# Log-softmax backward on one core: three tiles loaded, then three stored, on one queue; result in place of dy; stores of whole rows

**Chip, cores, metric.** One core of one Trainium2 chip, the pair's other core idle. The metric is device time in microseconds (us) of one execution, median of several runs. All runs compared here are of the fast state.

## The reference

```python
def reference(y, dy):                      # both (8, 1024, 8192) float32
    softmax_x = np.exp(y)
    sum_dy = np.sum(dy, axis=-1, keepdims=True)
    return (dy - softmax_x * sum_dy).astype(np.float32)
```

As a matrix that is 8192 rows of 8192 numbers: 64 tiles of 128 rows, 4 MiB each for y, dy and the result.

## The kernel before

```python
    yp = ctx.enter_context(tc.tile_pool(name="yp", bufs=3))
    dyp = ctx.enter_context(tc.tile_pool(name="dyp", bufs=2))
    op = ctx.enter_context(tc.tile_pool(name="op", bufs=2))
    # ... psum (2 buffers), stats; H = 4096, CD = 2048
    for i in range(n_tiles):
        # ...
        nc.sync.dma_start(out=dy_t[:], in_=dy_f[sl])
        nc.sync.dma_start(out=y_t[:], in_=y_f[sl])
        nc.vector.tensor_reduce(out=s_t[:], in_=dy_t[:], ..., negate=True)
        for h in range(n_half):
            o_t = op.tile([P, H], fp32)
            for q in range(n_q):
                # ... c = h * n_q + q; e_t in PSUM = exp(y_t[:, cs]) on ScalarE
                nc.vector.scalar_tensor_tensor(      # e_t * s_t + dy_t
                    out=o_t[:, q * CD : (q + 1) * CD], in0=e_t[:], scalar=s_t[:], in1=dy_t[:, cs], ...)
            nc.sync.dma_start(out=out_f[sl][:, h * H : (h + 1) * H], in_=o_t[:])
```

All DMAs go out from SyncE, in one order, on one queue. A scheduler settles that order; it isn't the source's. In the kernel before it is, from the second tile on: dy of tile i+1, the two half stores of tile i, y of tile i+1, dy of tile i+2, and so on.

## Time and profile before

| | before |
|---|---|
| time, median of 3 (range) | 1925.06 us (1923.62 to 1926.75) |
| moved | 805.3 MB: two thirds read, one third written |
| mean rate | 418 GB/s |
| DMA queue, share of 16 engines' time | 99.5% |
| VectorE, ScalarE busy | 59%, 25% |

The DMA bounds it: no compute engine is near full, and the queue's packets fill nearly all the time. The prediction below shows the lines.

Two orders of issue are told apart here by the **lead** of a transfer: the time from its issue on SyncE to its first packet on a DMA engine. The trace gives both ends. A short lead means that the queue was nearly empty when the transfer was put into it. The 16 engines don't run in step, so a lead has a value for the fastest engine (which comes first to the new transfer, so has the shortest) and for the slowest. The packet records carry no engine number. Packets are put to an engine by time: a packet starts some 3 ns before the end of the one ahead of it on the same engine. Where two engines end together this can mix them up, so figures by single engine are good to a few cases, not exact.

### The profile page before, as it was taken

The numbers are of one execution on the slowest core, as the hardware profiler recorded it, in microseconds if no ns is written. First come the engines' busy times: TensorE is split into PE (matmuls) and PEld (weight loads), VectorE is DVE, ScalarE is ACT, GpSimd is POOL, SyncE is SP. The second block draws the span as 40 slices with busy tenths as digits, with TensorE's granted clock in tenths as the row PEclk, the third lists the DMA queues.
The fourth block names the chain that finished last, engine by engine and source line by source line (L and its number), as shares of the span: only waits on it lengthen the run. The fifth ranks groups of instructions, "written<-read, shape, count | busy, mean of one in ns | idle before, by whom it ended". The sixth has DMA issues, their size and how long they took to land.

```text
span 1924.6 us, 1253 instructions
## 1 busy us (share of the span) xinstructions
DVE 1134.1 (59%) x320; ACT 477.5 (25%) x257; POOL 0.2 (0%) x4
## 2 busy tenths in 40 slices
DVE  5657556465564655756657556475564655646555
ACT  1322313223132131221322313223132231321312
POOL 0000000000000000000000000000000000000000
DMA  9999999999999999999999999999999999999997
GB/s 414 426 432 415 425 424 420 423 420 423 420 414 425 422 420 423 414 424 420 421 423 414 420 422 421 418 422 422 418 426 420 418 425 425 414 425 414 425 425 318
DMA packets 36874, 805.40 MB, mean 418 GB/s; under 512 B 4096, under 2 KB 4096, under 8 KB 4096
## 3 DMA queue, kind: packets, MB, share of 16 engines
q1 hardware_dynamic: 36864, 805.32, 99.5%
q14 instruction: 10, 0.08, 0.0%
HBM read 536.87 MB, written 268.44 MB: 418 GB/s over the span
## 4 chain that ended last, share of the span: by engine, by line
DMA 61%; DVE 29%; ACT 6%; issue 2%; SPq 1%; DVEq 0%; ACTq 0%
DMA y_t<-in_y_dram 61%; DVE o_t L70 29%; ACT e_t L67 6%; SPq L78 1%; DVEq L104 0%; ACTq L67 0%; SPq L51 0%; SPq L50 0%
## 5 line engine op out<-in xcount | busy, mean ns | idle before, releaser
L70 DVE SCALAR_TENSOR_TENSOR o_t<-e_t,s_t,dy_t 128x2048 f32<-128x2048 f32 x256 | 584.1, 2344 | 770.0 <-ACT e_t L67 770.0
L67 ACT ACTIVATE e_t<-y_t 128x2048 f32<-128x2048 f32 x256 | 476.2, 1877 | 1436.2 <-DMA y_t<-in_y_dram 1372.4
L53 DVE TENSOR_REDUCE s_t<-dy_t 128x1 f32<-128x8192 f32 x64 | 555.2, 8676 | 12.9 <-DMA dy_t<-in_dy_dram 12.9
L67 ACT ACT_TABLE_LOAD x1 | 1.3, 1283 | 0.7 <-PEq L93 0.7
L93 POOL MEMSET const-bfloat16-1.0<- 128x1 bf16 x1 | 0.1, 102 | 0.0
L93 POOL MEMSET const-uint8-127<- 128x1 uint8 x1 | 0.1, 102 | 0.0
L93 POOL MEMSET const-float32-0.0<- 128x1 f32 x1 | 0.1, 99 | 0.2 <-issue 0.2
L93 POOL MEMSET const-float32-1.0<- 128x1 f32 x1 | 0.1, 99 | 0.0
## 6 DMA issues: line engine op xcount, KB each, us to landing
dy_t<-in_dy_dram SPq DMA_DIRECT2D x64, 4096.0 KB, 27.8
y_t<-in_y_dram SPq DMA_DIRECT2D x64, 4096.0 KB, 18.3
out_dram<-o_t SPq DMA_DIRECT2D x128, 2048.0 KB, 8.7
```

Of the source, the lines that this page charges most:

```text
L53: nc.vector.tensor_reduce(out=s_t[:], in_=dy_t[:], axis=mybir.AxisListType.X, op=mybir.AluOpType.add, negate=True,)
L67: nc.scalar.activation(e_t[:], y_t[:, cs], mybir.ActivationFunctionType.Exp)
L70: nc.vector.scalar_tensor_tensor(out=o_t[:, q * CD : (q + 1) * CD], in0=e_t[:], scalar=s_t[:], in1=dy_t[:, cs], op0=mybir.AluOpType.mult, ...
L78: nc.sync.dma_start(out=out_f[sl][:, h * H : (h + 1) * H], in_=o_t[:])
L93: nc = _bacc.Bacc("TRN2", target_bir_lowering=False, num_devices=1)
```

## The change

The intent: fewer changes between loading and storing, larger store packets, no output buffers.

```diff
-    n_half = 2
-    ...
-    yp = ... bufs=3;  dyp = ... bufs=2;  op = ... bufs=2
+    BATCH = 3
+    dyp = ctx.enter_context(tc.tile_pool(name="dyp", bufs=BATCH + 1))
+    yp = ctx.enter_context(tc.tile_pool(name="yp", bufs=2))
...
+    first = n_tiles % BATCH
+    starts = [0] * bool(first) + list(range(first, n_tiles, BATCH))
+    for b, e in zip(starts, starts[1:] + [n_tiles]):
+        done = []
+        for i in range(b, e):
+            # load dy_t, load y_t, s_t = -sum(dy_t), as before
+            subtract_scaled_exp(nc, psum, y_t, dy_t, s_t[:], CD)   # writes into dy_t
+            done.append((sl, dy_t))
+        for sl, dy_t in done:
+            nc.sync.dma_start(out=out_f[sl], in_=dy_t[:])
```

More of the change, by code (lines that the diff above doesn't have):

```diff
@@ L8, with subtract_scaled_exp @@
 from concourse.bass import ts
+ACT_EXP = mybir.ActivationFunctionType.Exp
+ALU = mybir.AluOpType
+def subtract_scaled_exp(nc, psum, y_part, dy_part, neg_sum, width):
+    total = y_part.shape[-1]
+    for c in range(0, total, width):
+        e_t = psum.tile([128, width], mybir.dt.float32, name="e_t")
+        nc.scalar.activation(e_t[:], y_part[:, c : c + width], ACT_EXP)
+        nc.vector.scalar_tensor_tensor(
+            out=dy_part[:, c : c + width],
+            in0=e_t[:],
+            scalar=neg_sum,
+            in1=dy_part[:, c : c + width],
+            op0=ALU.mult,
+            op1=ALU.add,
+        )
 @with_exitstack
@@ L27 @@
     N, D = y_f.shape
-    assert N % P == 0, (N, P)
     n_tiles = N // P
-    n_half = 2
-    H = D // n_half
-    n_q = 2
-    CD = H // n_q
-    assert CD * 4 * 2 <= 16 * 1024, "psum budget"
-    yp = ctx.enter_context(tc.tile_pool(name="yp", bufs=3))
-    dyp = ctx.enter_context(tc.tile_pool(name="dyp", bufs=2))
-    op = ctx.enter_context(tc.tile_pool(name="op", bufs=2))
+    assert N == n_tiles * P
+    CD = 2048
+    BATCH = 3
+    dyp = ctx.enter_context(tc.tile_pool(name="dyp", bufs=BATCH + 1))
@@ L40 @@
+    yp = ctx.enter_context(tc.tile_pool(name="yp", bufs=2))
     psum = ctx.enter_context(tc.tile_pool(name="psum", bufs=2, space=bass.MemoryType.PSUM))
     stats = ctx.enter_context(tc.tile_pool(name="stats", bufs=8))
-    for i in range(n_tiles):
-        sl = ts(i, P)
-        dy_t = dyp.tile([P, D], fp32)
-        y_t = yp.tile([P, D], fp32)
-        s_t = stats.tile([P, 1], fp32)
-        nc.sync.dma_start(out=dy_t[:], in_=dy_f[sl])
-        nc.sync.dma_start(out=y_t[:], in_=y_f[sl])
-        nc.vector.tensor_reduce(
-            out=s_t[:],
-            in_=dy_t[:],
-            axis=mybir.AxisListType.X,
-            op=mybir.AluOpType.add,
-            negate=True,
-        )
-        for h in range(n_half):
-            o_t = op.tile([P, H], fp32)
-            for q in range(n_q):
-                c = h * n_q + q
-                cs = slice(c * CD, (c + 1) * CD)
-                e_t = psum.tile([P, CD], fp32)
-                nc.scalar.activation(
-                    e_t[:], y_t[:, cs], mybir.ActivationFunctionType.Exp
-                )
-                nc.vector.scalar_tensor_tensor(
-                    out=o_t[:, q * CD : (q + 1) * CD],
-                    in0=e_t[:],
-                    scalar=s_t[:],
-                    in1=dy_t[:, cs],
-                    op0=mybir.AluOpType.mult,
-                    op1=mybir.AluOpType.add,
-                )
-            nc.sync.dma_start(out=out_f[sl][:, h * H : (h + 1) * H], in_=o_t[:])
@@ new lines @@
+    first = n_tiles % BATCH
[3 more added lines that the diff above has]
+        for i in range(b, e):
+            sl = ts(i, P)
+            dy_t = dyp.tile([P, D], fp32, name="dy_t")
+            nc.sync.dma_start(out=dy_t[:], in_=dy_f[sl])
+            y_t = yp.tile([P, D], fp32, name="y_t")
+            nc.sync.dma_start(out=y_t[:], in_=y_f[sl])
+            s_t = stats.tile([P, 1], fp32, name="s_t")
+            nc.vector.tensor_reduce(
+                out=s_t[:], in_=dy_t[:], axis=mybir.AxisListType.X, op=ALU.add, negate=True
+            )
+            subtract_scaled_exp(nc, psum, y_t, dy_t, s_t[:], CD)
+            done.append((sl, dy_t))
+        for sl, dy_t in done:
+            nc.sync.dma_start(out=out_f[sl], in_=dy_t[:])
```

## The prediction

> **What bounds the kernel now.** First the page, busy shares and queue: is an engine near full, or the DMA?
>
> ```profile
> span 1924.6 us, 1253 instructions
> DVE 1134.1 (59%) x320; ACT 477.5 (25%) x257; POOL 0.2 (0%) x4
> DMA packets 36874, 805.40 MB, mean 418 GB/s; under 512 B 4096, under 2 KB 4096, under 8 KB 4096
> q1 hardware_dynamic: 36864, 805.32, 99.5%
> ```
>
> VectorE has 41% of the span free, ScalarE 75%. The one queue's packets fill 99.5% of 16 engines' time. So DMA bounds it, and only three things can help: fewer bytes, cheaper packets, or the 0.5%. The bytes stay: 64 tiles x 3 x 4 MiB = 805.3 MB.
>
> Second, the queue's waits and the DMA issues: does a late issue starve the queue?
>
> ```profile
> SPq L78 <- DVE o_t L70: 1736.8, 128, 27.1
> dy_t<-in_dy_dram SPq DMA_DIRECT2D x64, 4096.0 KB, 27.8
> y_t<-in_y_dram SPq DMA_DIRECT2D x64, 4096.0 KB, 18.3
> out_dram<-o_t SPq DMA_DIRECT2D x128, 2048.0 KB, 8.7
> ```
>
> SyncE sits 1737 us before stores, but that costs nothing in the steady state: a y load moves in some 9.7 us (below) and lands 18.3 us after its issue, so other packets were always ahead of it. "DMA y_t" as 61% of the chain means the same: compute waits for the queue.
>
> Third, bytes per stretch of time: first a stretch of pure loading, then three of the tail.
>
> ```profile
> 4.00:30.00 26.00, 14.16 (x4) 6.39 (x4) 0.00 (x0) 1.00 0.99 430
> 1903.00:1905.00 2.00, 0.00 (x0) 0.00 (x0) 0.00 (x0) 1.00 0.04 16
> 1905.00:1913.00 8.00, 5.06 (x3) 5.97 (x4) 0.00 (x0) 1.00 0.01 2
> 1913.00:1924.00 11.00, 4.07 (x2) 1.47 (x1) 0.00 (x0) 1.00 0.90 381
> ```
>
> The last two columns are DMA share and GB/s. Loads alone reach 430; the span's mean is 418. And from 1903 to 1913 the queue is empty: the last y has come, its tile is being computed, and nothing is left to move until its stores.
>
> Fourth, the trace's single DMA packets (start, duration, size), which no printed view shows; I sorted them by engine. A 32 KiB load packet takes 1213 ns and the next starts 1209.5 ns after it (27.1 GB/s per engine, 433 for 16). A 16 KiB store packet takes 611 ns, one every 607. But of each run of 16 store packets (two stores of half a row, 8 packets per engine each) the last is on average 400 ns too long, the one before 85, the third from the end 12; the first load packet after it is 116 too long. Small excesses and gaps at the same two borders of a cycle (stores to loads 0.02 us, loads to stores 0.06, the last load packets 0.04) bring it to **0.73 us per engine and change of direction and back**. Whole cycles agree: loads 19.58 us where 16 x 1.2095 = 19.35, stores 10.29 where 16 x 0.607 = 9.71, together 0.81 too long, the rest of it semaphore packets and single packets inside. Inside the runs nearly nothing is lost, not even at the border between the two half stores (0.3 ns). So part of the "99.5% busy" is packets that stand still while stores give way to loads. That is what there is to win.
>
> **What the Trainium skill says.** "DMA: Bandwidth & Descriptors", section "Where 436 GB/s comes from", puts the ceiling of 16 engines at 435.2 GB/s; the load runs at 433 agree, so within a run nothing is left. "HBM Reference", section "Specifications (TRN2)", says that a core streaming alone gets about 425 GB/s, bounded by its DMA engines; 418 here is below that, with loads and stores mixed. "DMA: Bandwidth & Descriptors", section "Queues, rings and completion order", says that on each DMA engine descriptors are consumed in ring order; the packets agree: each engine's runs of loads and stores follow the order of issue, so the program decides how often the direction changes. No page gives a cost for a change of direction; the 0.73 us is this trace's. The same page, section "Latency and other measured facts", puts an HBM access at 0.2 us on average and 2 us at high load; that the engine waits about one HBM read when it goes from reading SBUF to reading HBM would fit 0.73, but is only my reading.
>
> **The change part by part.**
> 1. Directions. Before, each tile is two loads, then its two half stores: 64 store runs, 63 of them followed by loads. After, the instruction order has one single tile, then 21 batches of three: 22 store runs, 21 followed by loads. 42 fewer x 0.73 = **30.6 us** off the path, as the queue is the path.
> 2. The tail. Before, the engines idle 9.6 us (largest gap per engine, mean of 16) between the last y packet and the last stores. After, when the last y is in, two stores (19.4 us) stand in the queue. The last tile needs 13.4 us from its last packet: 2.3 to the start of exp, 1.9 for exp, 9.13 for the four VectorE instructions (the trace's last tile: packets end at 1903.6, VectorE at 1917.1). So its store joins a queue with 6 us left: **9.6 us** saved.
> 3. Packets. 1024 store packets of 607 ns per engine become 512 of 32 KiB. If these go like loads (1209.5), 512 x (1214 - 1209.5) = **2.3 us**. 64 fewer semaphore packets per engine of some 6 ns: **0.4 us**.
> 4. In place. The result goes to dy's tile; same instruction, shapes and count (256 of 2344 ns). VectorE's 1134 us stay beside the transfers. Cost 0, if the waits hold, which I walk through, with 9.7 us per 4 MiB and time 0 at the last packet of a batch's first y: dy_b to 9.7, y_b 19.4, dy_c 29.0, y_c 38.7, stores a, b, c to 48.4, 58.1, 67.7. The issue of store c: 38.7 + 13.4 = 52.1, before 58.1: **6 us in hand**, the tightest place. The next dy_b needs store a complete (48.4 + 2.3 = 50.7, before 52.1), the next dy_c needs store b (60.4, with four transfers queued behind it by then). y_c waits for the exps of tile a (11 us after y_a; three transfers are queued). Store a then waits for VectorE at 13.4, store b at 32.8. VectorE: sum for c 32.8 to 41.5, exp for c ready at 42.9. Start: the first store is issued at 33.7 with dy and y of tile 1 queued to about 41. Nothing starves.
>
> Sum: 30.6 + 9.6 + 2.3 + 0.4 = 42.9; 1924.6 - 42.9 = 1881.7 in the profile, and some 0.5 more in the timed median (1925.06): **1882 us**, 2.2% faster, at 428 GB/s.
>
> **The rivals.**
> - Lost time goes with bytes stored or number of DMAs, not with changes of direction. Then only the tail and packet terms come: 1925 - 12 = 1913, within 2%. Against it: the clean inside of the runs, and the 0.3 ns at the half-store border, where a DMA ends and no direction changes. For it: nothing before has runs of more than 16 store packets.
> - The queue starves: SyncE issues in order, and y_c, store a and each dy wait in it for compute or for stores in place. Each us lost per batch costs 21 us; 2 us would eat the gain (1924). For it: only 6 us in hand, where the former kernel stored from buffers of its own. Against: the walk above, and stalls of 2 us wouldn't fit in its numbers.
> - The change of direction costs more after 12 MiB of stores than after 4 (a write backlog that must drain). At 1.5 us instead of 0.73 it costs 21 x 0.77 = 16 us: 1898, within 2%. Against: a backlog would lengthen packets through the run, and they stay at 611 up to the last three.
> - Less than thought remains: the engines drift apart less, and borders get cheaper. 1876.
>
> **Range and chances.** 2% faster is 1886.6, only 4.6 us above my sum, so the sizes matter, not the direction. The largest term (30.6) is a mean over 63 borders, and I give it 20% either way (6 us); the tail term is sure to 2 us. Range 1871 to 1897. Faster by over 2%: 0.68; within 2%: 0.31; slower: 0.01.
>
> **What would show each step.** Right: some 428 GB/s; no empty stretch between the last y and the last stores; the last store packets of a batch long by some 0.5 us and 21 such places, not 63; stores of 4096 KB landing 37, 28 and 18 us after issue in a batch (from the walk), so 28 as the median; q1 share still at 99%. Wrong: a DMA share below 0.9 inside batches (starving), store packets that lengthen within a run (writes saturate), a border that costs over 1 us, or a 32 KiB store packet well over 1213 ns.

## The result

The changed kernel takes **1871.67 us** (median of 4, 1871.40 to 1872.19) against 1925.34 us (4 runs) before. Ratio 0.972, interval 0.9706 to 0.9733: faster by 2.8%. A ratio is the mean time of one kernel's fast runs over that of the other's in the same rounds, so not quite the ratio of the medians quoted. The time lies inside the predicted range (1871 to 1897), at its lowest edge: the gain is 53.7 us where 43 were forecast.

The page of the changed kernel (span, engines, packets, queue):

```profile
span 1870.2 us, 1067 instructions
DVE 1136.0 (61%) x320; ACT 477.5 (26%) x257; POOL 0.2 (0%) x4
DMA packets 27656, 805.38 MB, mean 431 GB/s; under 512 B 3072, under 2 KB 3072, under 8 KB 3072
q1 hardware_dynamic: 27648, 805.32, 100.0%
```

The same bytes at 431 GB/s in place of 418, VectorE as before. The queue's share went from 99.5 to 100.0%: by this share there was half a per cent to win, and 2.8% was won. So this share doesn't tell how much can be won; more below.

Its waits of SyncE and its DMA issues (count, KB, median us from issue to landing):

```profile
SPq L75 <- DVE dy_t L20: 867.4, 64, 20.8
SPq L67 <- DMA y_t<-in_y_dram: 583.6, 21, 29.4
SPq L67 <- ACT e_t L19: 178.4, 21, 8.5
SPq L65 <- DMA out_dram<-dy_t: 100.8, 20, 5.7
dy_t<-in_dy_dram SPq DMA_DIRECT2D x64, 4096.0 KB, 45.2
y_t<-in_y_dram SPq DMA_DIRECT2D x64, 4096.0 KB, 36.3
out_dram<-dy_t SPq DMA_DIRECT2D x64, 4096.0 KB, 27.7
```

The price of working in place is there (SyncE waits 101 us for stores before it loads dy again), but it costs nothing, as every transfer is issued so long before its turn: 27.7 to 45 us to landing, where 4 MiB move in 9.7. In the kernel before, a half store landed 8.7 us after its issue, of which some 4.9 are its own packets and 0.35 the way from the last packet to the semaphore (median). Little is left, 3.3 us on the slowest engine and 1.0 to 1.5 on most of the others: it was issued when the queue was nearly dry.

Bytes per stretch at the end of the changed kernel (last columns DMA share, GB/s):

```profile
1838.00:1856.00 18.00, 11.80 (x5) 7.44 (x4) 0.00 (x0) 1.00 1.01 434
1856.00:1866.00 10.00, 0.00 (x0) 0.00 (x0) 0.00 (x0) 1.00 0.87 374
1866.00:1870.00 4.00, 0.00 (x0) 0.00 (x0) 0.00 (x0) 1.00 0.06 25
```

The empty 10 us between the last y and the last stores are gone, as forecast. In their place is a smaller loss: most engines end within 1 us of each other, but the last one 3.8 us after the middle one. In the kernel before, the empty stretch let the late engine catch up, and the last packets ended within 0.2 us of each other.

And the bubbles? Time by which single packets took longer than the usual 1213 ns (32 KiB) or 611 ns (16 KiB), added up, per engine, from the trace's packet records:

```
                  stretched packets   of which store packets
before                 44.9 us              34.5 us
changed                 4.5 us      (sizes are equal; last stores of runs: under 0.1 us)
```

By the prediction's rule, 21 changes of direction at 0.73 us should have left 15 us. They left almost nothing: over the 20 later batches together, the first load after the stores is too long by under 0.1 us per engine, and so is the last store. So a change from stores to loads is free in the changed kernel. It wasn't the change of direction that cost.

### The profile page after: what moved, and what is told of

The parts are those of the page before. It is cut to its first block, busy times and chain, and to the rows that moved or that the text cites. A ratio compares the mean times of both kernels' runs of the same rounds, so it can differ in the third digit from the quotient of the medians.

```text
span 1870.2 us, 1067 instructions
## 1 busy us (share of the span) xinstructions
DVE 1136.0 (61%) x320; ACT 477.5 (26%) x257; POOL 0.2 (0%) x4
## 4 chain that ended last, share of the span: by engine, by line
DMA 61%; DVE 13%; ACT 5%; SPq 1%; issue 0%; DVEq 0%; ACTq 0%
DMA y_t<-in_y_dram 61%; DVE dy_t L20 13%; ACT e_t L19 5%; SPq L65 1%; SPq L75 0%; DVEq L101 0%; ACTq L19 0%; SPq L67 0%
## 5 line engine op out<-in xcount | busy, mean ns | idle before, releaser
L20 DVE SCALAR_TENSOR_TENSOR dy_t<-e_t,s_t,dy_t 128x2048 f32<-128x2048 f32 x256 | 584.0, 2344 | 139.5 <-ACT e_t L19 139.5
## 6 DMA issues: line engine op xcount, KB each, us to landing
out_dram<-dy_t SPq DMA_DIRECT2D x64, 4096.0 KB, 27.7
```

The lines of the kernel that those rows point to most:

```text
L20: nc.vector.scalar_tensor_tensor(out=dy_part[:, c : c + width], in0=e_t[:], scalar=neg_sum, in1=dy_part[:, c : c + width], op0=ALU.mult, o ...
```

## The experiments

Twelve runs, three rounds each. Stretched packets and leads are of the one profiled execution of each run.

### First set: which part of the change is it?

**b1_32k**: whole-row stores, in place, but batches of one.

```diff
-    BATCH = 3
+    BATCH = 1
-    dyp ... bufs=BATCH + 1
+    dyp ... bufs=4
```

> The changed kernel with batches of one tile (dy in four buffers), stores still of whole rows, 32 KiB packets. 64 store runs of 8 packets per engine, as many changes of direction as in the kernel before. Theory P (the packet's size: a 16 KiB store packet ahead of loads leaves a bubble, a 32 KiB one doesn't): every border stays near the 0.09 us of the changed kernel, so 1872 + 42 x 0.09 + some 4 us of idle tail (only one store stands in the queue when the last y has come) = about 1879 us. Theory D (the number of changes of direction counts, and long runs make each cheap): 63 x 0.73 us come back, so about 1920 us.

Measured: 1874.3 us, ratio 0.9743. 64 changes of direction, no bubble (stretched packets 4.2 us).

**b3_16k**: batches of three, but half-row stores.

```diff
-            nc.sync.dma_start(out=out_f[sl], in_=dy_t[:])
+            for c in range(0, D, D // 2):
+                nc.sync.dma_start(out=out_f[sl][:, c : c + D // 2], in_=dy_t[:, c : c + D // 2])
```

> The changed kernel, batches of three, each store cut into two of half a row, so 16 KiB packets. Theory P: the last store packet of a run is 0.4 to 0.5 us too long again and the first load packet some 0.1, at 21 borders 0.73 x 21 = 15 us, and 2.3 us for the shorter packets: about 1889 us. Theory D: only the 2.3 us for shorter packets, about 1874 us.

Measured: 1876.5 us, ratio 0.9754; stretched packets 4.4 us. No bubble with 16 KiB either.

**b1_16k**: both at once, so in place is all that is left of the change.

> Batches of one and stores of half a row: the kernel before with the result written in place. Both theories: 63 borders at 0.73 us and an idle tail, 1920 to 1926 us. If writing in place itself were the gain, it would stay near 1875.

Measured: 1925.8 us (12 runs), ratio 1.0003; stretched packets 43.5 us. Working in place alone gives nothing.

**b3_rows**: batches of three; each store as two DMAs of 64 whole rows.

```diff
+            for r in range(0, P, P // 2):
+                nc.sync.dma_start(out=out_f[sl][r : r + P // 2], in_=dy_t[r : r + P // 2])
```

> Batches of three, each store cut into two DMAs of 64 whole rows: as many store DMAs (128) as in the kernel before, but 32 KiB packets. Theory P: as the changed kernel, 1872 to 1874 us, no bubble. If the number of store DMAs or the order of issue made the bubble rather than the packet, it would be as b3_16k.

Measured: 2165.8 us, ratio 1.127: far slower, which neither theory said. Two stretches of it, one with stores of 64 rows and one with loads alone (last columns DMA share, GB/s):

```profile
930.00:940.00 10.00, 8.59 (x4) 5.00 (x3) 0.00 (x0) 1.00 0.91 275
970.00:980.00 10.00, 1.87 (x1) 0.00 (x0) 0.00 (x0) 1.00 1.01 436
```

Loads run at 436, the stretch with 64-row stores at 275, and packets of 2.2 to 2.8 us appear (18% of all take over 1.3 us; one third of all are stores). The Trainium skill, "DMA: Bandwidth & Descriptors", section "Rules for kernel authors", says of two transfers to disjoint partition halves not to bother, since they serialize. The run agrees that nothing is gained, but it also loses, and why these packets take longer was not looked into. For the question of the bubble the run tells nothing.

So neither the packet's size (theory P) nor the number of direction changes (D): either part of the change removes all bubbles, and only with neither are they back. What b1_32k and b3_16k share, against b1_16k, is something the diff doesn't show: the scheduler settled on **another order of issue**, with more transfers ahead of each store and of the load behind it.

### Second set: the order of issue

**before_deep**: the kernel before, its buffers and half stores, with the loads of tile i+1 written ahead of the compute of tile i, so that SyncE issues dy and y of the next tile before this tile's stores.

```diff
+    loads(0)
     for i in range(n_tiles):
-        nc.sync.dma_start(out=dy_t[:], in_=dy_f[sl])
-        nc.sync.dma_start(out=y_t[:], in_=y_f[sl])
+        if i + 1 < n_tiles:
+            loads(i + 1)
+        dy_t, y_t = tiles.pop(i)
```

> The kernel before, with only the order of issue changed: dy and y of the next tile are issued ahead of this tile's two half stores; 16 KiB packets, 64 store runs, output buffers as before. Theory L (too late an issue: in the kernel before, the y load behind the stores is issued only 6.3 us before its first packet is due, and that isn't enough for the engines to go from stores to loads without a bubble; here it is some 16 us): no bubble and hardly an idle tail, 1872 to 1880 us. Theory B (the bubble belongs to short runs of 16 KiB store packets ahead of 32 KiB loads): bubbles as before, only the tail gained, 1913 to 1920 us.

Measured: **1876.05 us, ratio 0.975**, stretched packets 3.5 us. Its DMA issues:

```profile
dy_t<-in_dy_dram SPq DMA_DIRECT2D x64, 4096.0 KB, 33.6
y_t<-in_y_dram SPq DMA_DIRECT2D x64, 4096.0 KB, 42.8
out_dram<-o_t SPq DMA_DIRECT2D x128, 2048.0 KB, 24.4
```

Same packets, as many changes of direction, nothing in place, no batch: the order alone gives nearly the whole gain. A half store now lands 24.4 us after its issue in place of 8.7. But stores and loads both have longer leads here; which lead is it?

**before_slow**: one more VectorE instruction (128x1024, right values) at the end of each tile's compute, ahead of the second half store.

> The kernel before, with one more VectorE instruction of 128x1024 (some 1.2 us) at the end of each tile, writing values that are right. Theory L, with the loop y landed, compute, next issue, first packet as the true bound: each tile is 1.2 us longer, 64 x 1.2 = 77 us, about 2000 us, though VectorE still has a third of its time free. If the queue of DMA packets is the bound with a fixed bubble at each border (theory B), a part of the 6 us in hand is used and the time stays at 1925 us, at most 1 or 2 us more for the tail.

Measured: 1907.85 us, ratio 0.9912 (0.9897 to 0.9926). **More work, and 0.9% faster.** Theory L, with a loop through the compute as the bound, falls: it asked for 2000. Theory B asked for 1925; it falls too. Stretched packets: 29.9 us in place of 44.9.

**before_fast**: 1024 columns computed ahead of y's landing (wrong on purpose).

```diff
+            if h == 0:      # ahead of the exps: o_t[:, CD + 1024 :] from dy_t alone
+                nc.vector.scalar_tensor_tensor(out=o_t[:, CD + 1024 :], in0=dy_t[...], ..., in1=dy_t[...])
-                    out=o_t[:, q * CD : (q + 1) * CD], in0=e_t[:],
+                    out=o_t[:, q * CD : q * CD + w], in0=e_t[:, :w],      # w = 1024 for c == 1
```

> The kernel before, with 1024 of each tile's 8192 columns computed ahead of y's landing, without exp (wrong result on purpose), so the compute between the landing of y and the next issue is some 1.15 us shorter; order of issue, sizes and number of DMAs as before. Theory L: the lead of the y load grows from 6.3 to over 7 us, the bubble goes (in the first tiles of the kernel before, with leads of 7.0 to 7.4, it was 0.04 to 0.2 us), about 1885 us. Theory B: no change, 1924 us.

Measured: 1919.9 us, ratio 0.9979 (0.9967 to 0.9992); stretched packets 42.1 us. A miss for theory L (1885). The lead of y didn't grow as meant: only the first half store came earlier, the stretch from its issue to that of the second became longer (5.4 us in place of 4.5), and the engines drifted further apart.

**before_deep_slow**: before_deep with before_slow's extra instruction.

> Both: the loads issued ahead of the stores, and the extra VectorE instruction of some 1.2 us per tile. Theory L: the loop has slack now, the queue is the bound, and the extra work is hidden: within 3 us of the deep order alone. Theory B: as before_deep, so this run tells nothing more under it.

Measured: 1876.8 us, ratio 0.9752: in the deep order 1.2 us more compute per tile are hidden.

**Looking again.** For 60 tiles of the kernel before, take the lead of the first half store on the fastest engine and the stretched time around this tile's stores. They go together: correlation -0.92 (b1_16k -0.93, before_fast -0.90; before_slow -0.69 with all tiles, -0.97 without its first two). With the lead of y in its place it is much weaker (-0.2 to -0.4 in the kernel before, by how many of the first tiles are left out). Better still, by single engine: the lead of the first half store, and how long this engine's store packets of the tile and its next two loads were stretched.

```
lead of the first half store    before: engines x tiles, mean stretch
0.5 to 1.0 us                         172     1.00 us
1.0 to 1.5 us                         537     0.73 us
1.5 to 2.0 us                         150     0.32 us
3.0 to 4.0 us                          32     0.08 us
```

The rows from 2.0 to 3.0 us, left out above, have few cases and break the order: counted again, 8 cases at 2.0 to 2.5 us with 0.14 us and 21 at 2.5 to 3.0 us with 0.41. After the first tiles, nearly all leads over 2.5 us are of one single engine that runs some 2 us behind the rest, and its loss stands in the first load packet after the stores. So in this kernel the long leads prove little; the experiments below have to.

So a new theory, R: **the stores come too late.** When the stores are issued, most engines have some 1 to 1.5 us of load packets left. A picture of it, which no record shows: the side of an engine that reads ahead has nothing left to read, so the engine loses the distance between reading and writing, and pays at the next place where that distance is needed, where store packets give way to loads. What the records show is that most of the loss lies within the last store packet (0.42 us of 0.7).

It fits before_fast: the first half store's lead on the fastest engine grew to 1.5 us, but the second's fell from 1.5 to 1.1. In before_slow the first half store's lead grew to 2.2 us (from 1.0), yet where it was 2.0 to 2.5 us, engines still lost 0.43 us; the lead of the first half store alone doesn't explain that. There the second half store, held up by the extra instruction, had only 1.3 us. Sorted by the **shorter** of the two leads, the kernels come close together: at 1.5 to 2.0 us the stretch is 0.32 us in the kernel before, 0.27 in before_fast and 0.29 in before_slow (by the first lead alone 0.32, 0.62 and 0.83); at 1.0 to 1.5 us it is 0.73, 0.61 and 0.45.

Why did the leads grow in before_slow, where the compute is longer? Its engines stayed closer together: the last one ended a y load 0.5 us after the middle one (mean), in the kernel before 1.6 us. The compute waits for the last engine, and meanwhile the others work off the load packets behind. Why the engines stay together there isn't known.

### Third set: the lead of the stores against the lead of the loads behind them

**late_y**: stores as in the kernel before, the y load behind them held back by one more VectorE instruction.

```diff
-    yp ... bufs=3
+    yp ... bufs=1
+        # after the halves; y's only buffer is read here, so the next y waits for it
+        nc.vector.scalar_tensor_tensor(out=w_t[:], in0=y_t[:, :CD], scalar=s_t[:], in1=o_t[:, CD:], ...)
```

> The other way round, result right: the stores are issued as in the kernel before, but the y load behind them waits for one more VectorE instruction of 2.3 us (one y buffer), so its lead falls from 6.3 to some 4 us. Theory R: the stores' lead is unchanged, so the bubbles are, 1915 to 1930 us. Theory L: the bubble grows by what the lead loses, up to 2.3 us in each of 63 tiles: 1950 us or more.

Measured: 1928.3 us (20 runs), ratio 1.0021. The issues of one tile, kernel before, then late_y (start us, us, what):

```profile
924.93 4.86 SPq L78 DMA_DIRECT2D out_dram<-o_t  x2
929.89 0.57 SPq L51 DMA_DIRECT2D y_t<-in_y_dram  x1
```

```profile
928.22 4.86 SPq L79 DMA_DIRECT2D out_dram<-o_t  x2
935.16 0.34 SPq L52 DMA_DIRECT2D y_t<-in_y_dram  x1
```

From the first half store to the y load it is now 6.9 us, not 5.0, and the lead of y fell on the fastest engine from 6.3 to 4.4 us. The bubbles didn't grow (stretched packets 37.5 us), where theory L asked for 1950 us or more; the lead of the first half store is 1.2 us, a little longer than before. What late_y loses to the kernel before includes one gap of 8.3 us at its second tile, where its order of issue starts otherwise. Theory L is out.

**early_s**: stores some 2.3 us earlier (half of each stored half computed from dy alone, wrong on purpose), y held to its old time.

> Wrong result on purpose. Order of issue, sizes and number of DMAs as in the kernel before, but the second quarter of each half is computed from dy alone before y lands, so each half store waits for one VectorE instruction fewer after y and is issued some 2.3 us earlier; the y load behind the stores is held to its old time (one y buffer, read by the last VectorE instruction). Theory R (the stores come too late: at their issue the fastest engine has only about 1.0 us of loads left in the kernel before, its reading side runs dry although its packets show no gap, and the loss appears as the long last store packet): the lead of the stores grows to over 3 us, the bubbles go, about 1880 us with the idle tail still there. Theory L (the loads behind the stores come too late, 6.3 us ahead): their lead is unchanged, so are the bubbles, 1917 to 1925 us.

Measured: 1902.0 us, ratio 0.9885; stretched packets 30.2 us. Between the two theories. The trace is of the slowest of the four runs (1908.8 us; the others took 1901.4 to 1902.4). The reason shows in it: the engines drifted further apart (4.1 us between the first and the last to end a dy load, mean, in place of 2.3) until the fastest had only 1.4 us left when the stores came. By single engine the table holds: lead 0.5 to 1.0 us, stretch 1.02; 1.0 to 1.5, 0.68; 1.5 to 2.0, 0.23; 2.0 to 2.5, 0.06; 2.5 to 3.0, 0.02.

**early_s2**: three of four quarters of the stored tile from dy alone.

> Wrong result on purpose; early_s gained only half, as the engines drifted apart until the fastest had 1.4 us of loads left when the stores came. Here three of four quarters of the stored tile are computed from dy alone, before y lands, so the stores are issued 5 to 10 us earlier and no drift seen so far (7.7 us at most) can use it up; the y loads are still held back to the end of the compute, and in every second tile y follows the stores directly, with its old lead of 6 us. Theory R: no bubbles at either kind of border, some 1875 to 1882 us with an idle tail of up to 8 us. Theory L: bubbles of 0.7 us at the 31 borders with y behind the stores, 1897 us or more.

Measured: 1962.8 us, ratio 1.019. As a timing it failed both theories: the scheduler put dy of the next tile behind the stores in every second tile, VectorE (80% busy) then waited for dy and made the stores later still. It shows again how the order of issue can turn round.

But its packets do tell R from L, as two kinds of tile stand side by side in one run (leads on the fastest engine, means; stretch of the store packets and of the first load packets behind them, per engine and tile):

```
tiles                          lead of first half store   lead of the load behind   stretch
32, with y behind the stores            5.9 us                   4.3 us             0.00 us
31, with dy behind the stores           0.9 us                   5.9 us             1.0 us
```

The loss goes with the short lead of the stores, in spite of the longer lead of the load behind them: for R, against L.

**early_s3**: the same aim without these faults. ScalarE fills the stored halves from dy before y lands; only 512 columns of each wait for y; y of the next tile held to the end of the compute.

```diff
+            nc.scalar.activation(o_t[:], dy_t[:, h * H : (h + 1) * H], Exp)     # wrong on purpose
+        # exp of y's first 512 columns -> e0; 512 columns of each half from e0; then both stores
-                    out=o_t[:, q * CD : (q + 1) * CD],
+                    out=w_t[:],                                                # not stored
```

> Wrong result on purpose; early_s2 with its two faults taken away (there dy of the next tile fell behind the stores in the order of issue, and VectorE became late). Order of issue, sizes and number of DMAs as in the kernel before. The stored halves are filled from dy on ScalarE before y lands, and only 512 columns of each wait for y: both stores are issued some 3.4 us after y's last packet, so some 6 us ahead of the end of the dy load on the slowest engine, in place of 3.3. y of the next tile is held back to the end of the compute: lead 5.5 us, no more than in the kernel before. Theory R (the stores came too late): the bubbles go, and the idle tail shrinks from 9.6 to about 4 us, 1875 us, give or take 4. Theory L (the loads behind the stores came too late): bubbles as before, 1915 us or more.

Measured: **1879.1 us, ratio 0.9763**; stretched packets 5.1 us. Its issues of one tile, and its store landings:

```profile
931.20 1.04 SPq L83 DMA_DIRECT2D out_dram<-o_t  x2
941.35 0.34 SPq L52 DMA_DIRECT2D y_t<-in_y_dram  x1
```

```profile
out_dram<-o_t SPq DMA_DIRECT2D x128, 2048.0 KB, 13.9
```

The order, sizes and numbers of DMAs are those of the kernel before. The stores are issued 10 us ahead of y, with a lead of 3.5 us on the fastest engine and 7.7 on the slowest. The lead of y is 3.1 on the fastest engine, half of what it was. And the bubbles are gone. With late_y and the two kinds of tile in early_s2 this settles the matter between the two leads: it is the stores'.

| run | time, us | lead of first store, fastest / slowest engine | lead of the load behind the stores, fastest | stretched packets |
|---|---|---|---|---|
| before | 1925 | 1.0 / 3.3 us | 6.3 us | 44.9 us |
| b1_16k | 1926 | 1.0 / 3.3 | 6.3 | 43.5 |
| late_y | 1928 | 1.2 / 3.1 | 4.4 | 37.5 |
| before_fast | 1920 | 1.5 / 4.4 | 5.9 | 42.1 |
| before_slow | 1908 | 2.2 / 2.9 | 6.0 | 29.9 |
| early_s | 1902 | 1.4 / 5.4 | 4.8 | 30.2 |
| early_s3 | 1879 | 3.5 / 7.7 | 3.1 | 5.1 |
| b1_32k | 1874 | 4.0 / 7.7 | 13.3 | 4.2 |
| before_deep | 1876 | 15.1 / 19.0 | 19.7 | 3.5 |
| changed | 1872 | 24.3 / 27.2 | 14.2 | 4.5 |

(Leads are means over the tiles in the shallow orders, medians in the last three rows; in the changed kernel the last store of a batch has the shortest lead, 4.9 us. In before_slow and before_fast the second half store has the shorter lead, 1.3 and 1.1 us.)

## Why the prediction was right, and where it wasn't

**The bound.** Right that it is the queue. Wrong that SyncE's wait of 1737 us before stores "costs nothing in the steady state". The proof given was that a y load always had other packets ahead of it; the half stores, landing 8.7 us after issue, had only 1.0 to 1.5 us of them on most engines. That line was in the fence, and was not read to its end. A walk like that of part 4, made for the stores of the kernel before, would have shown it.

**Directions (30.6 us).** The step that failed: "part of the '99.5% busy' is packets that stand still while stores give way to loads", taken as a price of each change of direction, so that 42 fewer save 42 prices and 21 stay. The place of the loss was right and its size per tile too (0.73 us); its cause wasn't. It is the price of a store issued too late, and the changed kernel has no such store. So it fell at all 63 places: stretched packets 44.9 - 4.5 = 40.4 us, and the small gaps at the same borders (0.055 + 0.017 us, 63 times) 4.5 us. That is 45 us in place of 30.6, and explains why the time is at the edge of the range. Of the prediction's own signs, "the last store packets of a batch long by some 0.5 us and 21 such places" failed. That the time still fell inside the range, 0.7 us above its lower end, is partly luck: the largest term had the wrong cause, and the change happened to take away every late store.

**The tail (9.6 us).** Right: the queue doesn't run empty any more. Not foreseen: the last engine ends 3.8 us after the middle one. A misreading beside it: the "2.3 to the start of exp" after the "last packet" at 1903.6 was counted from the middle engine. One engine's last packet ended at 1905.7, and exp began 0.36 us later. So most of the 2.3 us was that one late engine, for which every tile's compute waits; this is a part of why the stores came late.

**Packets (2.7 us).** 32 KiB stores go at the loads' pace, as assumed. The sum of terms is 45 + 9.6 + 2.7 - 3.8 = 53.5, against 54.4 measured between the two profiled spans (1924.6 - 1870.2).

**In place, and the walk.** Right: VectorE's time is the same, the stores of a batch land 37.4, 27.7 and 18.0 us after issue (medians; 37, 28 and 18 were forecast), nothing starves. Only the wait for a store before a dy load, one per batch, is longer than in the walk (5.0 us on average, 5.7 at most), without harm.

**The rivals.** "Bytes stored or number of DMAs" and "dearer after 12 MiB" are out by b3_16k, b1_32k and the changed kernel. "The queue starves" was the right idea at the wrong kernel: it was the one before that starved, in a form without an empty stretch. The wild guess "borders get cheaper, 1876" was nearest.

**The reading of an HBM access** in the bubble ("the engine waits about one HBM read") isn't needed and got no support: the same borders are free when the stores came in time.

**What stays open.** That an engine's reading side runs ahead of its writing side is inferred; the packet records show no such side. The numbers show the dependence on the lead (0.7 us of loss at 1.0 to 1.5 us, next to none above 2.5 in early_s, early_s3 and b1_32k), not why the loss falls on the last store packet, nor why the late engine of the kernel before loses in its first load packet. Whether 32 KiB stores would pay the same at a lead of 1 us wasn't tried; b1_32k has 4.0, and no less than 2.5 ahead of a load. Why engines drift apart also stays open.

## What to carry to other kernels

Here a DMA queue at 99.5% was still starved. In such a case look at the time from issue to landing of each kind of transfer, take off its own packets and the way back, and if little is left, issue something ahead of it. Here that is one edit, the next tile's loads issued before this tile's stores (before_deep), worth 2.5% without batches, without larger stores and without in-place work; batches of three do the same in another way, and have no empty stretch at the end of the kernel, where before_deep's engines still idle some 3 to 7 us ahead of the last stores. When a change touches buffers, compare the order of issue of the two kernels first: it can move more than the change itself does.

## What the Trainium skill lacked or had wrong

- "DMA: Bandwidth & Descriptors", section "Rules for kernel authors", says under overlap to issue a DMA early. It lacks how early for a store behind loads: here, where the shorter lead of the two half stores was 1.0 to 1.5 us, an engine lost 0.73 us per tile, at 1.5 to 2.0 us 0.32, and in early_s at 2.5 to 3.0 us next to nothing (0.02).
- "Perfetto Trace Analysis", section "Identifying the Most-Contended Engine", calls the occupancy of the DMA misleading, because there are 16 engines. It lacks that packets themselves can be stretched, so that their share of the time hides the loss: it was 99.5% while 44.9 us of 1924.6 were packets stretched beyond their usual duration, and 100.0% in the changed kernel at 431 GB/s.
- "HBM Reference", section "Specifications (TRN2)", gives about 425 GB/s for a core alone. That is a little low here: the changed kernel, a third of it stores, ran at 431 over its whole span.
- "DMA: Bandwidth & Descriptors", section "Rules for kernel authors", on two partition halves: it lacks the price. When only the stores of the changed kernel are halved by rows (b3_rows), the time goes from 1871.7 to 2165.8 us, with 275 GB/s in a stretch of such stores.
- "DMA: Bandwidth & Descriptors", section "Latency and other measured facts", says that two engines are usually slower, and lays it, as a guess, to DMAs issued from GpSimd. It lacks that the 16 engines drift apart in a long stream issued from SyncE: between the first and the last engine to end the same DMA it was 0.5 us at the start of the changed kernel and 4.6 at its end.
